# Keeping the merged sum and two branch outputs of a hybrid decoder step in DRAM, with one tile pool for both lanes and gates ahead of projections in the last branch

## The chip, the core and the metric

The kernel runs on one core of one Trainium2 chip. The core has five engines with an instruction queue each: TensorE (PE, matmuls), VectorE (DVE), ScalarE (ACT), GpSimd (POOL) and SyncE (SP, which issues most DMAs). Each queue runs in order. The metric is the device time of one execution in microseconds; several executions are timed and their median is given. One execution is profiled, and all rows below come from that one.

## What is computed

One inference step of a two-layer decoder on 512 prompt tokens and 32 sample tokens (8 sequences of 4), which share all weights. In each layer four branches read one combined projection of the normalised input; each branch output (width 512) is gated, projected to 1024 and weighted, and the four are summed:

```python
h = rmsnorm(x, norm_g); z = h @ w_in          # columns split among all branches
y_conv, y_hg, y_mla, y_mem = ...              # short conv | HGRN2 | MLA over a paged cache | memory cross-attention
ys = jnp.stack([y_conv, y_hg, y_mla, y_mem], axis=2) * jax.nn.silu(sg)
proj = jnp.einsum('btnw,nwd->btnd', ys, w_bout)
merged = jnp.sum(jax.nn.sigmoid(mg) * proj, axis=2)
return x + merged @ w_o, ...
```

The keys and values of the memory branch come from `rmsnorm(mem) @ w_k` and `@ w_v` per layer; the MLA branch of the sample tokens reads 2048 cached positions per sequence through a page table.

## The kernel before

All activations are kept feature-major: 128 features on the partitions, 544 tokens (512 + 32) in the free dimension, in two halves of 272. Every large product is done in three float32r matmuls: a weight is split into `wh` (ACT copy) and `wl` (DVE subtract), an activation into a high and a low part (`Hh`/`Hl`, `ysh`/`ysl`, `Mh`/`Ml`), and high-high, high-low and low-high are accumulated.

The work of TensorE is a list of **items**, one weight tile each (`add`, `zi`): four `mk` and four `mv` (keys and values of the memory), then per layer the latent tiles, the queries, the conv tiles, and per branch four gates `sg` and eight pairs of `mg` (the gate of the merge) and `pj` (the projection), at last eight `wo`. A z item is 48 matmuls of 128x272, a `pj` 24. The three tiles of an HGRN head (hq, hf, hi) are put between pairs: heads 0 and 1 in the conv branch, heads 2 and 3 in the memory branch (`HG`). Counted from 0, item 57 is hq of head 2, items 68 to 70 are hq, hf and hi of head 3, and big matmul 2784 of the first layer is the first of item 70.

The main loop loads item i+2, splits item i+1, runs the deferred calls, runs the matmuls of item i with a step of **lane** a between its halves, evacuates its PSUM tile and makes a step of lane b. Lane a holds memory attention and HGRN, lane b MLA; both are generators whose small matmuls (`sm`, four PSUM tiles) fill in between the big ones (`big`, two PSUM tiles, so that item i+2 needs item i copied out). `drain` runs a lane to the point that an item needs.

Program order is not the final order: a scheduler moves instructions on each engine, and tiles come from rotating pools, so that an instruction which writes a new tile waits until an older tile of that pool is free. Pools here: `wrp` (3 raw weight tiles), `whp` (2 of `wh`, 2 of `wl`), `ep` (3 tiles e), `tpa` (13 tiles for lane a) and `tpb` (14 for lane b), and `kp` with single tiles, among them `M` (8 x 544, the merged sum, which also serves as X, the residual stream) and `ym`.

The places that the change touches: `ev_pj` makes the merged sum: the conv branch writes `M` on DVE, the others add to it on POOL. `split_merged` makes `Mh` and `Ml` from `M` ahead of the first `wo` item. `ev_out` adds the residual into X, stores it to DRAM (`x1`) for the next layer, and `xn_feed` squares and adds it for the norm; `xn_finish` gets the norm's factor (a short chain on POOL), makes the tiles e, and splits them into `Hh` and `Hl`. `mem_load` and `mem_split` load the memory rows and split them (`ra`) for `mk` and `mv`. The outputs of memory attention are in `ym`, those of HGRN in one lane tile per head, until the `sg` items gate them. For the sample tokens of MLA, eight jobs per quarter load the cached latents (`tb<-in_latT`, four DMAs each), split them into `rb` and run their small matmuls; those with `S`, `m`, `QR` and `cnew` belong to their softmax.

Of the kernel before, what the change touches and what calls it, by code (L numbers as in the profile page):

```python
# [19 lines left out]
P = 128  # L20
# [18 lines left out]
TA, TB = 13, 14  # L39
# [97 lines left out]
def hybrid_kernel(ctx: ExitStack, tc: tile.TileContext, a, o):  # L137
# [7 lines left out]
    ep = pool("ep", 3)  # L145
    tps = {"a": pool("tpa", TA), "b": pool("tpb", TB)}
# [10 lines left out]
    def t(name=None):  # L157
        n = name or lane[0]
        return tps[n].tile([P, T], F32, tag="t" + n, name="t" + n)

    def tr():
        return tps[lane[0]].tile([P, T], F32R, tag="t" + lane[0], name="r" + lane[0])
# [59 lines left out]
    x1 = dp.tile([P, KD, T], F32, name="x1")  # L222

# [205 lines left out]
    def xn_finish(l):  # L429
# [6 lines left out]
        rs = rstd_small(ps[:, 0:5], 1024, alloc=sl_, eng=G)  # L436
# [10 lines left out]
        for d in range(KD):  # L447
            h = e_()
            stt(h, X[:, d, :], g_("norm", 8 * l + d), r, ALU.mult, ALU.mult)
# [178 lines left out]
    def ev_sg(l, n, i):  # L628
        def run(it):
# [10 lines left out]
            else:  # L640
                y = {CONV: lambda: st[l]["cv"], HGRN: lambda: st[l]["yh", i], MEM: lambda: st[l]["ym"][:, i, :]}[n]()
                stt(g, g, 0.5, y, ALU.mult, ALU.mult)
# [16 lines left out]
    def ev_mg(l, n, d):  # L659
        def run(it):  # L660
            x = e_()
            act(v2(x), ps2(it), AF.Tanh, scale=0.5)
            st[l]["tm"] = x
        return run

    def ev_pj(l, n, d):
        def run(it):
            x = st[l]["tm"]
            if n == CONV:
                if d == 0:  # L670
                    st[l]["M"] = kp.tile([P, KD, T], F32, tag="M", name="M")
                stt(v2(st[l]["M"][:, d, :]), v2(x), 1.0, ps2(it), ALU.add, ALU.mult)
            else:
                stt(v2(x), v2(x), 1.0, ps2(it), ALU.add, ALU.mult)
                tt(st[l]["M"][:, d, :], st[l]["M"][:, d, :], x, ALU.add, eng=G)
        return run

    def split_merged(l):
        M = st[l]["M"]
        Mh = kp.tile([P, KD, T], F32R, tag="H1", name="Mh")  # L680
        Ml = kp.tile([P, KD, T], F32R, tag="H2", name="Ml")
        for d in range(KD):
            act(Mh[:, d, :], M[:, d, :], AF.Copy)
            tt(Ml[:, d, :], M[:, d, :], Mh[:, d, :].bitcast(F32), ALU.subtract)
        st[l]["Ms"] = (Mh, Ml)

    def ev_out(l, d):
        def run(it):
            if d == 0:
                X = kp.tile([P, KD, T], F32, tag="M", name="X")  # L690
                if l + 1 < NL:
                    st[l + 1]["X"] = X
                st[l]["Xn"] = X
# [961 lines left out]
```

## Time and profile before

| | |
|---|---|
| median of 3 runs | 1739.29 us (1735.88 to 1740.36) |
| the profiled execution | 1735.38 us, of which the span is 1733.2 us |
| PE busy | 1704.0 us (98%), 14042 matmuls; weight loads 1642.6 us (95%) |
| DVE busy | 1079.2 us (62%) |
| ACT busy | 849.7 us (49%) |
| POOL busy | 333.2 us (19%) |
| DMA | 201.12 MB, 116 GB/s on average |

The span runs from the first to the last instruction; the 2.2 us that lie around it belong to the execution's time. A busy share is an average over the whole span. Where a row of the trace has an idle time in brackets, the engine stood still before that instruction, and the name behind the arrow is what ended the wait.

### The profile page before, as it was taken

Reading aid. Unit: us, or ns where it says so; the run is one execution under the profiler, and the core shown is the slowest. Engines: PE = TensorE matmul, PEld = TensorE weight load, DVE = VectorE, ACT = ScalarE, POOL = GpSimd, SP = SyncE. Lnnn points to the kernel's source line nnn. Section 1 sums busy time; section 2 is a strip of 40 time slices with the busy share of each in tenths; the row PEclk is TensorE's granted clock in tenths of the full one; section 3 lists DMA queues with packets and bytes.
Section 4 is the critical chain, followed back from the end, with each engine's and each line's share of the span. In section 5 each row is a group of like instructions: output and inputs, shape, how many; then the busy total and the mean of one; then the engine's idle time right before and its main releaser. Section 6 shows DMA issues by size and latency. Waiting matters only on the chain.

```text
span 1733.2 us, 36030 instructions
## 1 busy us (share of the span) xinstructions
PE 1704.0 (98%) x14042; PEld 1642.6 (95%) x14042; DVE 1079.2 (62%) x2468; ACT 849.7 (49%) x1651; POOL 333.2 (19%) x366
## 2 busy tenths in 40 slices
PE   7999999999999999999999999999999999999999
PEld 5899899999999999999989998999999999999999
DVE  7565654768787976332465756556787888744333
ACT  6646444565757563222346554355656665523231
POOL 5010001112243322101130100001133433221110
PEclk9999999999999999999999999999999999999999
DMA  6322542334334443223453135323343434333233
GB/s 233 116 62 77 172 132 81 106 113 128 118 120 133 132 127 105 90 74 111 153 169 106 53 98 178 105 78 115 115 141 106 143 110 128 110 101 87 83 113 121
DMA packets 106828, 201.12 MB, mean 116 GB/s; under 512 B 13921, under 2 KB 48098, under 8 KB 106658
## 3 DMA queue, kind: packets, MB, share of 16 engines
q1 hardware_dynamic: 99346, 177.79, 32.9%
q0 software_dynamic: 7168, 20.98, 4.1%
q8 instruction: 111, 1.82, 0.4%
q14 instruction: 59, 0.48, 0.1%
q10 hardware_dynamic: 144, 0.04, 0.0%
HBM read 186.72 MB, written 12.04 MB: 115 GB/s over the span
## 4 chain that ended last, share of the span: by engine, by line
PE 86%; DVE 6%; ACT 4%; issue 2%; DMA 1%; SPq 1%; POOL 0%; ACTq 0%; DVEq 0%
PE big L171 66%; PE sm L171 18%; DVE ta L180 1%; DVE wl L180 1%; DMA tb<-in_latT 1%; ACT ta L174 1%; ACT tb L174 1%; ACT wh L174 1%; DVE e L177 1%; ACT L174 1%; SPq L1244 0%; PE sm L1203 0%; PE sm L981 0%; DVE Ml L180 0%; DMA ta<-in_memT 0%
## 5 line engine op out<-in xcount | busy, mean ns | idle before, releaser
L171 PE MATMUL big<-Hh,wh 128*128 128x272 f32 x2528 | 744.3, 295 | 0.6 <-ACT Hh L174 0.2
L171 PE MATMUL big<-Hh,wl 128*128 128x272 f32 x2528 | 736.6, 291 | 2.9 <-DVE wl L180 2.9
L171 PE MATMUL big<-Hl,wh 128*128 128x272 f32 x2528 | 735.0, 291 | 2.2 <-DVE Hl L180 1.8
L171 PEld LDWEIGHTS big<-Hh,wh 128*128 128x128 f32 x2528 | 477.5, 189 | 8.7 <-issue 5.6
L171 PEld LDWEIGHTS big<-Hl,wh 128*128 128x128 f32 x2528 | 477.7, 189 | 6.2 <-DVE Hl L180 2.8
L171 PEld LDWEIGHTS big<-Hh,wl 128*128 128x128 f32 x2528 | 477.0, 189 | 5.5 <-DVE wl L180 4.3
L174 ACT ACTIVATE wh<-wr 128x1024 fp32r<-128x1024 f32 (+1 forms) x246 | 232.8, 946 | 460.2 <-PE big L171 382.3
L180 DVE TENSOR_TENSOR wl<-wr,wh 128x1024 fp32r<-128x1024 f32 (+1 forms) x246 | 273.3, 1111 | 272.2 <-ACT wh L174 271.2
L174 ACT ACTIVATE tb<-sm 128x256 f32<-128x256 f32 (+6 forms) x380 | 140.2, 398 | 81.2 <-PE sm L171 66.4
L180 POOL TENSOR_TENSOR M<-M,e 128x544 f32<-128x544 f32 x48 | 96.9, 2019 | 358.4 <-DVE e L177 349.2
L171 PE MATMUL big<-ysh,wh 128*128 128x272 f32 x512 | 149.6, 292 | 0.0
L171 PE MATMUL big<-ysh,wl 128*128 128x272 f32 x512 | 148.6, 290 | 0.0
L171 PE MATMUL big<-ysl,wh 128*128 128x272 f32 x512 | 148.4, 290 | 0.0
L174 ACT ACTIVATE ta<-ta 128x544 f32<-128x544 f32 (+3 forms) x180 | 96.0, 538 | 55.6 <-DVE ta L180 46.4
L171 PE MATMUL sm<-ta 128*128 128x128 f32 (+6 forms) x1424 | 122.5, 279 | 0.3
L180 DVE TENSOR_TENSOR ta<-ta 128x256 f32<-128x256 f32 (+3 forms) x248 | 111.9, 488 | 8.8 <-ACT ta L174 8.1
L171 PEld LDWEIGHTS sm<-ta 128*32 128x32 f32 (+1 forms) x1424 | 101.2, 147 | 9.0 <-issue 2.8
L171 PE MATMUL sm<-Rh,rb 128*128 128x272 f32 x512 | 105.9, 295 | 2.0 <-DVE S L1276 2.0
L1222 POOL DMA_INDIRECT tb<-in_rop,row4i x64 | 71.3, 1113 | 189.9 <-PE sm L171 94.9
L189 DVE TENSOR_REDUCE s<-tb 128x8 f32<-128x512 f32 (+1 forms) x150 | 100.8, 674 | 4.5 <-ACT tb L174 4.4
L1222 POOL DMA_INDIRECT tb<-in_lat,row4i x64 | 68.8, 1074 | 158.4 <-PE sm L171 63.6
L171 PEld LDWEIGHTS big<-ysh,wh 128*128 128x128 f32 x512 | 96.6, 189 | 0.4 <-issue 0.4
(242 smaller groups left out, 2556.1 us busy)
## 6 DMA issues: line engine op xcount, KB each, us to landing
wr<-in_w_in SPq DMA_DIRECT2D x158, 512.0 KB
wr<-in_wb SPq DMA_DIRECT2D x64, 256.0 KB
tb<-in_latT SPq DMA_DIRECT2D x256, 64.0 KB
ta<-in_mkT SPq DMA_DIRECT2D x32, 256.0 KB
ta<-in_mv SPq DMA_DIRECT2D x32, 256.0 KB
wr<-in_wo SPq DMA_DIRECT2D x16, 512.0 KB
ta<-in_shg SPq DMA_DIRECT2D x16, 256.0 KB
out_hgs<-ta SPq DMA_DIRECT2D x16, 256.0 KB
```

The lines of the kernel that those rows point to most:

```text
L171: return TE.matmul(out, lhsT, rhs, start=start, stop=stop)
L174: S.activation(out, in_, f, **k)
L177: V.scalar_tensor_tensor(out=out, in0=in0, scalar=sc, in1=in1, op0=op0, op1=op1)
L180: (eng or V).tensor_tensor(out=out, in0=in0, in1=in1, op=op)
L189: V.tensor_reduce(out=out, in_=in_, op=op, axis=AX.X, **k)
L1222: G.indirect_dma_start(out=out, out_offset=None, in_=a[src], in_offset=bass.IndirectOffsetOnAxis(ap=idx, axis=0))
```

## The change

The merged sum leaves the on-chip memory: it is kept in a DRAM tensor `md`. Each branch's `ev_mg` loads the sum so far into a tile e, `ev_pj` adds to it and a deferred call stores it again. The outputs of memory attention and HGRN go to DRAM too (`ymd`, `yhd`), and `load_y` fetches them ahead of the `sg` items. The tiles `M` and `ym` are gone; in their place there are six tiles e instead of three, and the two lane pools become one of 27. X is a list of eight tiles of that pool. The norm's factor is made on DVE. In the MLA branch all eight `mg` items come first, then all eight `pj` items, and each merged tile gets its last sum and its split right behind its `pj` item, so `split_merged` is gone.

```diff
-TA, TB = 13, 14
+NT = 27
...
-    ep = pool("ep", 3)
-    tps = {"a": pool("tpa", TA), "b": pool("tpb", TB)}
+    ep = pool("ep", 6)
+    lp = pool("lp", NT)
...
     def t(name=None):
         n = name or lane[0]
-        return tps[n].tile([P, T], F32, tag="t" + n, name="t" + n)
+        return lp.tile([P, T], F32, tag="t", name="t" + n)
...
+    md = dp.tile([P, KD, T], F32, name="md")
+    ymd = dp.tile([P, 4, T], F32, name="ymd")
+    yhd = dp.tile([P, 4, T], F32, name="yhd")
...
-        rs = rstd_small(ps[:, 0:5], 1024, alloc=sl_, eng=G)
+        rs = rstd_small(ps[:, 0:5], 1024, alloc=sl_)
...
-                y = {CONV: lambda: st[l]["cv"], HGRN: lambda: st[l]["yh", i], MEM: lambda: st[l]["ym"][:, i, :]}[n]()
-                stt(g, g, 0.5, y, ALU.mult, ALU.mult)
+                stt(g, g, 0.5, st[l]["y"] if n != CONV else st[l]["cv"], ALU.mult, ALU.mult)
...
     def ev_mg(l, n, d):
         def run(it):
-            x = e_()
+            x = t("b") if n == MLA else e_()
             act(v2(x), ps2(it), AF.Tanh, scale=0.5)
-            st[l]["tm"] = x
+            st[l]["tm", d] = x
+            if n != CONV:
+                m = st[l]["mo", d] = t("b") if n == MLA else e_()
+                SY.dma_start(out=m, in_=md[:, d, :])
         return run
 
     def ev_pj(l, n, d):
         def run(it):
-            x = st[l]["tm"]
-            if n == CONV:
-                if d == 0:
-                    st[l]["M"] = kp.tile([P, KD, T], F32, tag="M", name="M")
-                stt(v2(st[l]["M"][:, d, :]), v2(x), 1.0, ps2(it), ALU.add, ALU.mult)
-            else:
-                stt(v2(x), v2(x), 1.0, ps2(it), ALU.add, ALU.mult)
-                tt(st[l]["M"][:, d, :], st[l]["M"][:, d, :], x, ALU.add, eng=G)
-        return run
-
-    def split_merged(l):
...
+            x = st[l].pop(("tm", d))
+            stt(v2(x), v2(x), 1.0, ps2(it), ALU.add, ALU.mult)
+            if n != CONV:
+                tt(x, x, st[l].pop(("mo", d)), ALU.add, eng=V if n == MLA else G)
+            if n != MLA:
+                defer(1, lambda: SY.dma_start(out=md[:, d, :], in_=x))
+                return
+            if d == 0:
+                st[l]["Ms"] = (kp.tile([P, KD, T], F32R, tag="H1", name="Mh"), kp.tile([P, KD, T], F32R, tag="H2", name="Ml"))
+            Mh, Ml = st[l]["Ms"]
+            act(Mh[:, d, :], x, AF.Copy)
+            tt(Ml[:, d, :], x, Mh[:, d, :].bitcast(F32), ALU.subtract)
+        return run
 
     def ev_out(l, d):
         def run(it):
...
+            xo = t("b")
+            if l + 1 < NL:
+                st[l + 1].setdefault("X", []).append(xo)
...
-            act(ym[:, :, qb * P:(qb + 1) * P], ps.rearrange("p (h q) -> p h q", h=4), AF.Copy)
+            y = t()
+            act(y[:, 0:TP], ps, AF.Copy)
+            defer(1, lambda: SY.dma_start(out=ymd[:, :, qb * P:(qb + 1) * P], in_=y[:, 0:TP].rearrange("p (h q) -> p h q", h=4)))
...
         stt(ob, ob, g_("hgn", 4 * l + h), r, ALU.mult, ALU.mult)
-        st[l]["yh", h] = ob
+        defer(1, lambda: SY.dma_start(out=yhd[:, h, :], in_=ob))
...
+    def load_y(l, name, flag, src, i):
+        def run():
+            if i == 0:
+                drain(l, name, flag)()
+                run_deferred()
+            y = e_()
+            SY.dma_start(out=y, in_=src[:, i, :])
+            st[l]["y"] = y
+        return run
...
                 zi(l, ("mg", n, d), ev_mg(l, n, d))
-                add(l, ("pj", n, d), a["wb"][l, n, d], 512, proj_mm(l), ev_pj(l, n, d))
+                if n != MLA:
+                    add(l, ("pj", n, d), a["wb"][l, n, d], 512, proj_mm(l), ev_pj(l, n, d))
+            if n == MLA:
+                for d in range(8):
+                    add(l, ("pj", n, d), a["wb"][l, n, d], 512, proj_mm(l), ev_pj(l, n, d))
...
-        for tag in ("Q", "ym", "ysh", "ysl"):
+        for tag in ("Q", "ysh", "ysl"):
...
-        X = st[0]["X"] = kp.tile([P, KD, T], F32, tag="M", name="X0")
+        X = st[0]["X"] = [t("b") for _ in range(KD)]
```

The same matmuls stand in the new program, 12654 in both; SP has 1146 DMAs where it had 1016. What moves on the engines is shown at three places.

ACT in the memory branch, first layer, around the copy of HGRN head 3's hq (item 68) out of PSUM, `ta<-big`. In the kernel before:

```order
L174 ACTIVATE ta<-sm,epsc 128x272 x2
L174 ACT_TABLE_LOAD
L174 ACTIVATE ta<-ta 128x544
L174 ACT_TABLE_LOAD
L174 ACTIVATE ta<-ta 128x544
L174 ACTIVATE tb<-sm 128x256
L174 ACTIVATE ta<-ta 128x544
L174 ACTIVATE tb<-sm 128x256 x4
L174 ACTIVATE rb<-tb 128x512
L174 ACTIVATE wh<-wr 128x1024
L174 ACTIVATE ta<-big 128x544
L174 ACTIVATE S<-S 128x272
```

In the changed kernel; the row right ahead of these is `wh<-wr 128x1024`, the weights of item 71, whose buffer is that of item 69:

```order
L174 ACTIVATE ta<-sm,epsc 128x272
L174 ACT_TABLE_LOAD
L174 ACTIVATE ta<-ta 128x544
L174 ACT_TABLE_LOAD
L174 ACTIVATE ta<-ta 128x544 x2
L174 ACTIVATE rb<-tb 128x512
L174 ACTIVATE tb<-sm 128x256 x5
L174 ACTIVATE S<-S 128x272
L174 ACTIVATE rb<-tb 128x512
L174 ACTIVATE tb<-sm 128x256 x4
L174 ACTIVATE tb<-sm 128x128
L174 ACTIVATE ta<-big 128x544
```

The copy stood behind the weights of item 70, and stands now behind those of item 71, the norm of the head before (the two table loads) and the ACT rows of two latent jobs. The second layer has the same.

PE at the same place. In the kernel before, `big<-Hh,wh` in the seventh row is the first matmul of item 70, and 9 small matmuls stand between it and item 69:

```order
L171 MATMUL sm<-Rh_105,rb 128x272 x2
L171 MATMUL sm<-Rl_107,rb 128x272
L171 MATMUL sm<-Rh_105,rb 128x272 x2
L171 MATMUL sm<-Rl_107,rb 128x272
L171 MATMUL sm<-Rh_105,rb 128x272 x2
L171 MATMUL sm<-Rl_107,rb 128x272
L171 MATMUL big<-Hh,wh 128x272
L171 MATMUL big<-Hl,wh 128x272
```

In the changed kernel 46 small matmuls stand between the two, of which these are the last 27, and then item 70:

```order
L171 MATMUL sm<-Rl_104,rb 128x272
L171 MATMUL sm<-m,ones 128x16
L171 MATMUL sm<-tb,S 32x128 x16
L171 MATMUL sm<-cnew,S 32x128
L171 MATMUL sm<-Rh_102,rb 128x272 x2
L171 MATMUL sm<-Rl_104,rb 128x272
L171 MATMUL sm<-Rh_102,rb 128x272 x2
L171 MATMUL sm<-Rl_104,rb 128x272
L171 MATMUL sm<-Rh_102,rb 128x272 x2
L171 MATMUL sm<-Rl_104,rb 128x272
L171 MATMUL big<-Hh,wh 128x272
L171 MATMUL big<-Hl,wh 128x272
```

The small matmuls are the same ones; those that stood among the big matmuls of items 66 to 69 have gathered ahead of item 70. At item 59 there is a shorter such run, of 15.

ACT at the layer change, where the last output items are followed by `mk` and `mv` of the second layer (`e<-X` or `e<-tb` is the square for the norm). In the kernel before:

```order
L174 ACTIVATE e<-X 128x544
L174 ACTIVATE wh<-wr 128x1024
L174 ACTIVATE e<-X 128x544
L174 ACTIVATE wh<-wr 128x1024 x4
L174 ACTIVATE ta<-big,rmem 128x512
L174 ACTIVATE tb<-big,rmem 128x512
```

In the changed kernel:

```order
L174 ACTIVATE e<-tb 128x544
L174 ACTIVATE wh<-wr 128x1024
L174 ACTIVATE e<-tb 128x544
L174 ACTIVATE ra<-ta,gn 128x256 x8
L174 ACTIVATE wh<-wr 128x1024 x3
L174 ACTIVATE tb<-sm 128x512
```

The split of the memory rows, `ra<-ta,gn`, which stood in the HGRN branch, has moved behind the square of the last X tile; its low parts, on DVE, likewise stand behind that tile's addition and a `wl`.

## Rows read from the trace of the kernel before

**Rows 1.** The page: busy time by engine, DMA bytes, the chain by line.
```profile
PE 1704.0 (98%) x14042; PEld 1642.6 (95%) x14042; DVE 1079.2 (62%) x2468; ACT 849.7 (49%) x1651; POOL 333.2 (19%) x366
...
DMA packets 106828, 201.12 MB, mean 116 GB/s; under 512 B 13921, under 2 KB 48098, under 8 KB 106658
...
PE big L171 66%; PE sm L171 18%; DVE ta L180 1%; DVE wl L180 1%; DMA tb<-in_latT 1%; ACT ta L174 1%; ACT tb L174 1%; ACT wh L174 1%; DVE e L177 1%; ACT L174 1%; SPq L1244 0%; PE sm L1203 0%; PE sm L981 0%; DVE Ml L180 0%; DMA ta<-in_memT 0%
```

**Rows 2.** Waits of PE: waiting line, releaser, us in total, times, longest.
```profile
PE big L171 <- ACT ra L174: 6.8, 1, 6.8
...
PE sm L171 <- DVE S L1276: 2.0, 2, 1.7
```

**Rows 3.** Windows: length, busy us (instructions) by engine, granted clock, DMA share, GB/s.
```profile
26.20:33.00 6.80, 6.75 (x21) 5.79 (x22) 3.90 (x8) 1.01 (x2) 5.19 (x17) 0.50 0.36 139
...
510.00:560.00 50.00, 50.00 (x424) 49.45 (x423) 39.43 (x110) 32.26 (x64) 16.96 (x20) 1.00 0.51 149
```

**Rows 4.** Timeline of ACT at items 68 and 69: start, us, instruction, [idle before].
```profile
525.08 1.07 ACT L174 ACTIVATE ta<-sm,epsc 128x272 f32<-128x272 f32 x2 [0.32 <-PE sm L171]
526.17 1.28 ACT L174 ACT_TABLE_LOAD   x1
527.46 0.66 ACT L174 ACTIVATE ta<-ta 128x544 f32<-128x544 f32 x1
528.14 1.28 ACT L174 ACT_TABLE_LOAD   x1
...
530.81 1.34 ACT L174 ACTIVATE tb<-sm 128x256 f32<-128x256 f32 x4
532.05 0.62 ACT L174 ACTIVATE rb<-tb 128x512 fp32r<-128x512 f32 x1
532.57 1.05 ACT L174 ACTIVATE wh<-wr 128x1024 fp32r<-128x1024 f32 x1
533.52 0.61 ACT L174 ACTIVATE ta<-big 128x544 f32<-128x544 f32 x1
...
539.56 0.28 ACT L174 ACTIVATE tb<-sm 128x128 f32<-128x128 f32 x1 [3.21 <-PE sm L171]
```

**Rows 5.** Timeline of DVE in the same stretch.
```profile
534.35 0.43 DVE L180 TENSOR_TENSOR S<-S,sm 128x272 f32<-128x272 f32 x1
...
536.43 0.62 DVE L189 TENSOR_REDUCE m<-S 128x16 f32<-128x272 f32 x1
```

**Rows 6.** Timelines at the layer change: PE, ACT, DVE.
```profile
875.49 0.63 PE L171 MATMUL big<-wh,ra 128*128 128x512 f32 x2
...
876.58 0.64 ACT L174 ACTIVATE e<-X 128x544 f32<-128x544 f32 x1
...
875.69 0.72 DVE L177 SCALAR_TENSOR_TENSOR X<-big,e 128x544 f32<-128x544 f32 x1 [3.80 <-PE big L171]
876.70 1.23 DVE L180 TENSOR_TENSOR wl<-wr,wh 128x1024 fp32r<-128x1024 f32 x1 [0.29 <-ACT wh L174]
```

**Rows 7.** Timelines of ACT and DVE in the HGRN branch: the split of memory.
```profile
621.82 0.90 ACT L174 ACTIVATE ra<-ta,gn 128x256 fp32r<-128x256 f32 x2
...
623.89 0.48 DVE L177 SCALAR_TENSOR_TENSOR ra<-ta,gn,ra 128x256 fp32r<-128x256 f32 x1
```

**Rows 8.** Timelines of PE and DVE at the first output item.
```profile
829.48 0.40 PE L171 MATMUL big<-Ml,wh 128*128 128x272 f32 x1 [0.78 <-DVE Ml L180]
...
826.90 4.42 DVE L180 TENSOR_TENSOR Ml<-M,Mh 128x544 fp32r<-128x544 f32 x5
```

**Rows 9.** Timeline of PE at the start.
```profile
24.62 0.73 PE L171 MATMUL big<-wh,ra 128*128 128x512 f32 x2 [2.00 <-ACT wh L174]
26.25 1.01 PE L171 MATMUL sm<-ones,tb 128*128 128x1 f32 x4 [0.89 <-DVE tb L180]
```

**Rows 10.** Pieces of the chain, in order of time: start, us, what.
```profile
469.94 3.24 DMA tb<-in_latT
...
700.43 45.24 PE big L171 x360
```

More of the change, by code (lines that the diff above doesn't have):

```diff
@@ L158, in t @@
         n = name or lane[0]
-        return tps[n].tile([P, T], F32, tag="t" + n, name="t" + n)
+        return lp.tile([P, T], F32, tag="t", name="t" + n)
     def tr():
-        return tps[lane[0]].tile([P, T], F32R, tag="t" + lane[0], name="r" + lane[0])
+        return lp.tile([P, T], F32R, tag="t", name="r" + lane[0])
     e_ = lambda: ep.tile([P, T], F32, tag="e", name="e")
@@ L448, in xn_finish @@
             h = e_()
-            stt(h, X[:, d, :], g_("norm", 8 * l + d), r, ALU.mult, ALU.mult)
+            stt(h, X[d], g_("norm", 8 * l + d), r, ALU.mult, ALU.mult)
             act(Hh[:, d, :], h, AF.Copy)
@@ L712, in lane_a @@
         KT, Vt = st[l]["KT"], st[l]["Vt"]
-        ym = st[l]["ym"] = kp.tile([P, 4, T], F32, tag="ym", name="ym")
         def p_s(qb):
@@ L831, in lane_a @@
         TE.transpose(ps[:, 0:P], acc[:, 0:P], ident)
-        act(ym[:, :, TP:T], ps[:, 0:P].rearrange("p (h t) -> p h t", h=4), AF.Copy)
+        y = t()
+        act(y[:, 0:P], ps[:, 0:P], AF.Copy)
+        SY.dma_start(out=ymd[:, :, TP:T], in_=y[:, 0:P].rearrange("p (h t) -> p h t", h=4))
         st[l]["mem_done"] = True
@@ L1457, in hybrid_kernel, with branch @@
             zi(l, ("sg", CONV, i), ev_sg(l, CONV, i))
-        def branch(n, before=None, after=None):
+        def branch(n, before=None):
             for d in range(8):
@@ L1476, in hybrid_kernel @@
         for d in range(8):
-            add(l, ("wo", d), a["wo"][l, d], 1024, out_mm(l), ev_out(l, d), pre=(lambda l=l: split_merged(l)) if d == 0 else None)
+            add(l, ("wo", d), a["wo"][l, d], 1024, out_mm(l), ev_out(l, d))
         if l + 1 < NL:
@@ L1533, in hybrid_kernel @@
         load(3)
-        X = st[0]["X"] = kp.tile([P, KD, T], F32, tag="M", name="X0")
+        X = st[0]["X"] = [t("b") for _ in range(KD)]
         for d in range(KD):
-            SY.dma_start(out=X[:, d, :], in_=a["xT"][:, d, :])
+            SY.dma_start(out=X[d], in_=a["xT"][:, d, :])
         for i in range(4, 8):
@@ L1542, in hybrid_kernel @@
         for d in range(KD):
-            defer(1 + d // 2, lambda d=d: xn_feed(0, d, X[:, d, :]))
+            defer(1 + d // 2, lambda d=d: xn_feed(0, d, X[d]))
         defer(2, setup)
```

17 lines of the change are left out of this document (2 added, 15 removed).

## Prediction

> **What bounds the kernel now.** I read the page first [rows 1]: TensorE (PE) is busy 1704.0 of 1733.2 us, and the chain that ended last is 66% big and 18% small matmuls, so only some 29 us of the span are not matmuls. The list of PE's waits [rows 2] says where: 6.8 us before the first one, then small change, among it two for the sample scores `S`; the split of the merged sum, `Ml`, makes two more [rows 8]. A page like this says that an edit can gain little, and that it costs whatever new waits it puts into PE's order. Nor does the diff touch what PE computes: the matmuls are the same in number and shape. So I went through the order of the instructions for places where PE must now wait for something that used to be early, and costed each from the timeline of the stretch in which it stood before.
>
> **Part 1, one tile pool: an evacuation that comes late (term A).** In the memory branch the three gates of HGRN head 3 (hq, hf, hi) are items 68, 69 and 70. The two big PSUM buffers alternate, so item 70 can't start before item 68 has been copied out, by ScalarE (ACT) into a tile of lane a. In the kernel before, that copy is the row at 533.52, a microsecond after item 69's start freed the weights of the wh at 532.57, and the whole stretch is dense: PE is busy 50.00 of 50.00 us [rows 3, 4]. In the changed kernel the order shows ACT's copy (`ta<-big`) twelve rows later, behind the norm of the head before and the ACT work of two paged-attention jobs, and PE's row shows the counterpart: 46 small matmuls in a row stand between the end of item 69 and item 70, where before it was nine. The tile that the copy writes now comes from the pool that both lanes share; whatever the reason, both queues run in order, so item 70 waits for that copy.
>
> How long? The first ACT row of the group is a wh that needs item 69's buffer, so nothing of it starts before PE has finished item 69; call this T. From below, ACT's own work: wh 1.06, half of the pair at 525.08 (0.5), two table loads 2.56, three `ta<-ta` of 0.66, two rb of 0.62, nine tb at 1.34 for four (3.0), 0.28 and the copy 0.61 make 11.2; neighbours overlap by some 0.1 each, so about 10 [rows 4]. The 46 matmuls fill part of it: 33 of 272 columns at 0.126 (45.24 us for 360, [rows 10]), 17 of 128 at half of that, a few tiny ones: 5.3 us. That leaves 4.7. From the other side, the same chain was run in the kernel before, hidden: from the norm's scaling at 525.08 to `tb<-sm` at 539.56 + 0.28 it took 14.8 us, because the steps go back and forth: ACT to VectorE (DVE; the add into S at 534.35, the maximum at 536.43), to PE (ACT's last row waited 3.21 for it) and back [rows 4, 5]. The first 0.5 of this lies ahead of T and the copy's 0.6 comes on top, 14.9; less 5.3 is 9.6. In the chain before, PE's big matmuls and a wl held it up by perhaps 2, and a wh of 1 and an rb of 0.7 are now in it that weren't, so I take 9.0, near the measured chain, with 4.7 and 12 as ends (12 if the latent load of the last job, which now stands behind a weight load that itself waits for item 69's buffer, is the later one: 2.3 for the weights, about 2 to issue, 3.24 to land [rows 10], then 1.3 of splitting, some 9 us, so it should be just hidden). Both layers have the place: **A = +18 (9.4 to 24)**.
>
> The same happens on a small scale at item 57 (hq of head 2): 15 small matmuls ahead of item 59, the copy behind a wh and one tb. After T that is 1.06 + 0.33 + 0.61 = 2.0 of ACT against 1.65 of PE, plus PSUM hand-offs: 1.5 each, **B = +3.0 (0.8 to 8)**. And the first loads of the cached memory keys stand behind the stores of the memory output: a store waits for its copy, then 0.3 to issue and 3.24 to land [rows 10], against some 3.4 us of matmuls up to the first use: 1.2 each, **C = +2.4 (0 to 6)**.
>
> **Part 2, the layer change (term D).** Before, the memory rows of the second layer were loaded and split in the HGRN branch (ACT at 621.82, DVE at 623.89 [rows 7]), and PE went from the last output matmul straight into `big<-wh,ra` at 875.49 [rows 6]. Now the tiles come free only with the last output items: the split stands behind X7 and its square on ACT (end 877.2) and behind X7 and a wl on DVE (end 877.9) [rows 6]. The first half of ra takes 0.45 more on ACT, its low part 0.48 on DVE [rows 7]: second matmul at 878.4, a stall of 2.7. Then the six h tiles ahead of Hl, which six e buffers allow, push two wl of 1.23 behind them; by the same rows PE waits 1.5 and 3.2 there, but the waits of before in this stretch (2 us) and 2 us of the norm, now on DVE instead of GpSimd (POOL), come back: **D = +3.2 (1 to 9)**.
>
> **Part 3, what it gains.** The split of each merged tile follows its projection, so the `Ml` waits go: PE stood 0.78 in front of one [rows 8] and some 0.4 in front of another, 1.2 per layer. DVE has five of them in one run of 4.42 us there [rows 8]; spread over the projections it needs 0.72 + 0.71 + 0.71 + 0.68 = 2.8 per 3.0 us of PE, nearly full, so I keep 1.0 each: **E = -2.0 (-2.5 to +0.5)**. At the start the norm leaves POOL and the squares no longer wait for e buffers; the last Hl comes about 2 us earlier, though the first ra now stands behind two more wh: **F = -2.0 (-4 to +2.5)**. The stores and reloads in DRAM themselves I cost at nothing: some 130 transfers of about 0.27 MB, 35 MB on 201 [rows 1], each with 6 us or more of other items between landing and use; the adds stay on POOL except in the last branch.
>
> **Part 4, the clock (term G).** After waits of 2.00 and 0.89 us in a row [rows 9] the granted clock was 0.50 for 6.8 us [rows 3], half of 2.4 GHz, which cost 3.4. Nothing in the kernel before has a gap as long as the new ones of A. The Trainium skill (TensorE: Matmul & The Clock Gate, Part 1: The HAM clock gate) has half rate as the state of an idle engine, lifted by activity; the rows at the start agree (0.50), and by it each of the two waits of A would be followed by a full spell, +6.8 in all. In A the PE is not idle but runs small matmuls in bursts, and its half clock is partly hidden behind the same chain, so I take 2 for each: **G = +4 (0 to 10, with the layer change)**.
>
> The small waits for S and the like shift with the small matmuls (2.0 us over two places [rows 2]); I take **H = -1 (-4 to +4)**.
>
> **Sum.** 18 + 3.0 + 2.4 + 3.2 - 2.0 - 2.0 + 4 - 1 = +25.6 on the profiled execution's 1735.38 us, so 1761.0. That execution lies 3.9 us below the median of the three runs (1739.29), and the changed kernel is timed like the median: 1739.3 + 25.6 = 1764.9, **about 1765 us**.
>
> **The rivals.**
> (1) Not slower: the long run of small matmuls is no wait. If ACT and DVE were well ahead when PE reaches T (because PE had already been held up earlier), the copy would come right after the run. Against it: the wh at the head of the group needs item 69's buffer, and ACT's own 10 us stand behind it. It would take A down to at most its lower end, 9.4, with B, C and G at zero, D at 1, E and F at -6.5 and H at -4: 1739 or a little less. It decides the sign from A below some 4 to 5 us per layer on. 0.08.
> (2) Faster: the shared pool and the six e buffers let the lanes run ahead, the run of 46 costs nothing, and the waits beyond the first 6.8 [rows 2] go in part. What is there to be had is 29 - 6.8 = 22 us at most, plus the half clock at the start; a third of it gives 1731. Against it: PE was dense already in the stretches where the lanes are heaviest [rows 3]. 0.04.
> (3) Much slower: the 130 DMAs more on SP's queue, which are in order and wait for POOL adds, hold the latent loads behind them; each job then adds its landing [rows 10] to PE's wait. Four more such waits of 3.3 us per layer give 1791. For it: in the second half of the memory branch four latent loads stand directly behind one weight load. Against: they are issued during the wait of A itself. 0.10.
> (4) Slower clock: after both waits of A and at the layer change a spell like the one at the start [rows 3] follows, and nothing hides it: G = 3 x 3.4 = 10.2, 1771. For it: each of these waits is as long as the 2.9 us at the start or longer, give or take 0.2. Against: PE works in between, and ACT and DVE catch up meanwhile. 0.20. It is what the page on TensorE named above, in the Trainium skill, would have.
>
> **How the numbers follow.** Forecast 0.58: with A between 5 and 12 per layer and the rest around the values above, 1750 to 1781, in which rival 4 lies too. Rivals 1 and 2 and most of rival 3 lie outside, so about 0.8 is held: range **1750 to 1781**. A measurement of this kernel can tell some 0.3% (5.2 us) from no change: faster 0.04 (rival 2), the same 0.07 (most of rival 1), slower 0.89.
>
> **What would show it.** A: in the profile after, PE's list of waits has two groups (near 545 and near 1410 us) in which waits for ACT copies (`tb`, `ta`), S and m stand between small matmuls, together 8 to 11 us each, and the copy `ta<-big` stands right ahead of item 70. If PE is dense there, A is wrong and with it the sign. D: a wait of some 2.7 us for ra at the layer change. E: no wait for `Ml`. G: a granted clock near 0.5 behind these waits. F: the last `Hl` before 52 us. If the time comes out slower with PE dense at A, rival 3 has to show as waits for tb and rb elsewhere in the branches.

## The result and the profile after

The changed kernel takes 1776.88 us (median of four runs, 1775.55 to 1779.11), the kernel before on the same chip 1737.72: a ratio of 1.0225, 95% interval 1.0205 to 1.0246. It is slower by 39 us in the median and by 44 in the two profiled executions.

The page of the kernel after, busy times and DMA:

```profile
span 1777.3 us, 36288 instructions
PE 1718.1 (97%) x14042; PEld 1654.8 (93%) x14042; DVE 1092.0 (61%) x2502; ACT 863.9 (49%) x1659; POOL 289.6 (16%) x326
DMA packets 129390, 236.79 MB, mean 133 GB/s; under 512 B 17025, under 2 KB 55298, under 8 KB 129218
```

Against [rows 1] the span has grown by 44.1 us. PE has the same 14042 matmuls and is busy 14.1 us longer, so they ran at a lower clock for a time (the granted clock is 0.986 on average, where it was 0.997); and it stands still for 59.2 us instead of 29.2. The waits of PE in the kernel after (engine, what it waited for, total us, times, longest us), to be held against [rows 2]:

```profile
PE big L171 <- DVE wl L180: 17.4, 10, 4.1
PE sm L171 <- DVE S L1277: 14.4, 5, 6.2
PE big L171 <- ACT ra L174: 14.0, 2, 11.7
PE big L171 <- ACT e L174: 3.7, 4, 1.4
PE big L171 <- DVE Hl L180: 2.6, 2, 1.5
PE big L171 <- DVE ra L177: 1.5, 2, 1.1
```

Four things are new: two waits of 6.2 us for `S`, a first matmul at 11.7 us instead of 6.8, long waits for `wl`, and waits for `e`; `Ml` [rows 8] is gone. To see where the 44 us lie, I took the start of each big matmul (they are the same 10080 in the same order) in both traces and compared stretch by stretch:

| big matmuls | what is there | longer by, us | predicted |
|---|---|---|---|
| up to 840 | start, first memory reads of layer 1 (F, half of C) | 5.7 | -0.8 |
| 840 to 4656 and 5600 to 9696 | branches of both layers (A, B, G, H, half of C) | 13.0 + 17.0 | 25.2 |
| 4656 to 4720, 9696 to 9760 | split of the merged tiles (E) | -2.5 | -2.0 |
| 4720 to 5600 | layer change (D) | 10.5 | 3.2 |
| sum | | 43.8 | 25.6 |

These are two single executions, and not all parts are equally sure. The runs below that leave a place as it is in the kernel after (1, 3, 8, 9 and 10 for the start, 1, 3, 8 and 9 for the layer change) show 2.6 to 6.0 us up to 840 and 8.3 to 9.8 us at the layer change; the loss from 2592 to 3300, which holds term A, is 11.5 to 12.1 us in the first layer in the runs that keep it (1, 4, 6 and 10).

**Term A in the rows.** PE after item 69 (start, us, form, idle before it and what ended the idle):

```profile
546.65 0.29 PE L171 MATMUL sm<-Rl,rb 128*128 128x272 f32 x1
553.12 1.97 PE L171 MATMUL sm<-QR,tb 128*128 128x64 f32 x8 [6.19 <-DVE S L1277]
554.88 0.55 PE L171 MATMUL sm<-m,ones 128*128 128x16 f32 x2
...
560.88 0.29 PE L171 MATMUL big<-Hh,wh 128*128 128x272 f32 x1
```

The last of these rows is item 70; from item 69 to it the trace has 79 small matmuls, nine in the kernel before. And ACT in the same stretch:

```profile
544.81 1.05 ACT L174 ACTIVATE wh<-wr 128x1024 fp32r<-128x1024 f32 x1
...
546.32 1.28 ACT L174 ACT_TABLE_LOAD   x1
...
548.28 1.28 ACT L174 ACT_TABLE_LOAD   x1
549.58 1.34 ACT L174 ACTIVATE ta<-ta 128x544 f32<-128x544 f32 x2
...
551.35 1.19 ACT L174 ACTIVATE tb<-sm 128x256 f32<-128x256 f32 x4
...
559.75 0.28 ACT L174 ACTIVATE tb<-sm 128x128 f32<-128x128 f32 x1 [0.98 <-PE sm L171]
559.92 0.62 ACT L174 ACTIVATE ta<-big 128x544 f32<-128x544 f32 x1
```

The copy of item 68 (`ta<-big`, at 533.52 in [rows 4]) now comes at 559.92, behind the norm with its table loads and the work of the jobs, and item 70 starts 0.3 us after it has ended. PE's wait is named after `S`, but what it waited for is this chain: `tb<-sm`, which frees the small PSUM tiles, stands behind the table loads. The same wait returns at 1432 us in the second layer. By stretch (us; busy time and instructions of PE, PEld, DVE, ACT, POOL; granted clock; DMA share; GB/s):

```profile
550.00:552.00 2.00, 0.00 (x0) 0.00 (x0) 0.98 (x2) 1.97 (x6) 0.00 (x0) 0.86 0.61 186
552.00:553.00 1.00, 0.00 (x0) 0.00 (x0) 1.00 (x4) 0.53 (x2) 0.00 (x0) 0.50 0.06 21
...
556.00:557.00 1.00, 1.00 (x6) 1.00 (x5) 0.59 (x2) 1.00 (x3) 0.00 (x0) 0.50 0.87 307
...
558.00:559.00 1.00, 1.00 (x24) 0.97 (x27) 0.69 (x4) 0.47 (x2) 0.00 (x0) 0.86 0.38 120
...
1429.00:1438.00 9.00, 5.73 (x32) 5.67 (x36) 6.72 (x18) 5.30 (x14) 0.00 (x0) 0.50 0.40 124
```

The granted clock falls to 0.50 (1.2 GHz) while PE stands still, stays there while it works through most of the small matmuls, and is back at 2.4 GHz before item 70. The last row is the second layer: there it is low for longer, 10 us in all instead of 7, behind a wait of the same 6.19 us.

**A second late evacuation.** At items 62 and 64 PE waits for the copies of the gates two items earlier, 1.35 and 0.5 us, and then 2.2 us for a `wl`. ACT and PE at the first of these:

```profile
479.03 1.28 ACT L174 ACT_TABLE_LOAD   x1
480.32 0.62 ACT L174 ACTIVATE e<-big 128x544 f32<-128x544 f32 x1
```

```profile
481.00 0.39 PE L171 MATMUL big<-Hh,wh 128*128 128x272 f32 x1 [1.35 <-ACT e L174]
```

The copy stands behind a table load of lane a, though the tile e that it writes doesn't come from the shared pool.

**The layer change** [rows 6, 7]. PE in the kernel after:

```profile
895.39 0.49 PE L171 MATMUL big<-wh,ra 128*128 128x512 f32 x1 [2.25 <-ACT ra L174]
896.95 0.79 PE L171 MATMUL big<-wh,ra 128*128 128x512 f32 x1 [1.07 <-DVE ra L177]
...
917.45 0.50 PE L171 MATMUL big<-wl,ra 128*128 128x512 f32 x1 [1.07 <-DVE wl L180]
...
924.57 0.80 PE L171 MATMUL big<-wl,ra 128*128 128x512 f32 x1 [4.05 <-DVE wl L180]
```

Ahead of the third of these rows, DVE has:

```profile
911.36 4.26 DVE L177 SCALAR_TENSOR_TENSOR e<-tb,gn 128x544 f32<-128x544 f32 x6
...
916.18 1.22 DVE L180 TENSOR_TENSOR wl<-wr,wh 128x1024 fp32r<-128x1024 f32 x1
```

PE stands 3.3 us for `ra`, then twice for `wl`, the first of which DVE makes behind six h tiles in a row. **The start:** ACT has two more `wh` ahead of the first `ra`, and the second of them waits for its weights:

```profile
10.20 1.06 ACT L174 ACTIVATE wh<-raw 128x1024 fp32r<-128x1024 f32 x1 [2.35 <-DMA raw<-in_wk]
11.16 2.49 ACT L174 ACTIVATE ra<-ta,gn 128x256 fp32r<-128x256 f32 x6
```

### The profile page after: what moved, and what is told of

It is laid out like the page before. It is cut to its first block, busy times and chain, and to the rows that moved or that the text cites. A ratio compares the mean times of both kernels' runs of the same rounds, so it can differ in the third digit from the quotient of the medians.

```text
span 1777.3 us, 36288 instructions
## 1 busy us (share of the span) xinstructions
PE 1718.1 (97%) x14042; PEld 1654.8 (93%) x14042; DVE 1092.0 (61%) x2502; ACT 863.9 (49%) x1659; POOL 289.6 (16%) x326
## 4 chain that ended last, share of the span: by engine, by line
PE 88%; ACT 5%; DVE 4%; issue 2%; DMA 1%; SPq 0%; DVEq 0%; ACTq 0%
PE big L171 67%; PE sm L171 19%; ACT L174 1%; ACT ta L174 1%; DVE wl L180 1%; ACT wh L174 1%; DVE e L177 1%; DVE ta L180 1%; ACT tb L174 1%; PE sm L1204 0%; PE sm L739 0%; PE sm L982 0%; DMA raw<-in_wk 0%; PE sm L1285 0%; PE sm L784 0%
## 5 line engine op out<-in xcount | busy, mean ns | idle before, releaser
L171 PEld LDWEIGHTS big<-Hh,wh 128*128 128x128 f32 x2528 | 478.9, 189 | 11.3 <-issue 4.6
L180 DVE TENSOR_TENSOR wl<-wr,wh 128x1024 fp32r<-128x1024 f32 (+1 forms) x248 | 279.5, 1127 | 245.8 <-ACT wh L174 242.6
L171 PE MATMUL sm<-Rh,rb 128*128 128x272 f32 x512 | 109.7, 301 | 0.0
L174 ACT ACTIVATE ta<-sm 128x512 f32<-128x512 f32 (+5 forms) x130 | 53.8, 429 | 99.3 <-PE sm L171 50.5
L171 PEld LDWEIGHTS big<-ysh,wl 128*128 128x128 f32 x512 | 96.4, 188 | 3.5 <-DVE wl L180 3.5
L180 POOL TENSOR_TENSOR e<-e 128x544 f32<-128x544 f32 x32 | 61.4, 1919 | 226.0 <-DVE e L177 186.9
```

The lines of the kernel that those rows point to most:

```text
L171: return TE.matmul(out, lhsT, rhs, start=start, stop=stop)
L174: S.activation(out, in_, f, **k)
L180: (eng or V).tensor_tensor(out=out, in0=in0, in1=in1, op=op)
```

## The experiments

Three theories stood against each other. **O:** with one pool, the instructions that write new tiles of both lanes come out in the order in which the program asks for the tiles, so that one lane stands behind the other. (That the scheduler goes by this order is inferred; the runs test what follows from it.) **S:** 27 tiles are too few for both lanes and X. **R:** the stores and reloads in DRAM hold up SP's queue. Ratios are to the kernel before, run on the same chip as each experiment.

| kernel | median, us | ratio (95% interval) |
|---|---|---|
| after | 1776.9 | 1.0225 (1.0205 to 1.0246) |
| after, 36 tiles | 1772.7 | 1.0208 (1.0191 to 1.0225) |
| after, two lane pools | 1735.3 | 0.9997 (0.9987 to 1.0006) |
| after, two lane pools, three e | 1733.2 | 0.9982 (0.9973 to 0.9991) |
| after, pool for the gates' copies | 1759.5 | 1.0139 (1.0122 to 1.0157) |
| after, X in its own tile | 1764.2 | 1.0163 (1.0146 to 1.0180) |
| after, both of these | 1747.3 | 1.0070 (1.0054 to 1.0085) |
| after, pool for the norm's tiles | 1779.8 | 1.0240 (1.0218 to 1.0263) |
| after, filler matmuls | 1772.3 | 1.0210 (1.0193 to 1.0227) |
| after, last branch in pairs | 1780.7 | one run, no interval |
| before, one pool | 1762.4 | 1.0156 (1.0140 to 1.0172) |
| before, one tile from the other pool | 1734.6 | 0.9992 (0.9983 to 1.0002) |
| before, last branch changed | 1732.4 | 0.9983 (0.9974 to 0.9992) |

**1. More tiles.**

```diff
-NT = 27
+NT = 36
```

> The changed kernel with 36 tiles in the one pool instead of 27. Theory O (handing out): the two lanes' tiles come from one pool in the order in which the program asks for them, whatever the number, so the copy of item 68 stays behind the ACT work of the paged-attention jobs and the rows ra stay behind X: 1777 us, give or take 3, with the same wait of some 6.2 us before the first matmul of item 70 in both layers and the first matmul near 11.7 us. Rival S (scarcity): 27 slots are too few for both lanes and eight X tiles; with nine more the late copy and the late split go, 1777 - 26 (stretch of items 68 to 70) and up to - 16 more (start, layer change): 1735 to 1751. Rival R (traffic): the stores and reloads in DRAM and their place in SP's queue hold PE up; nothing changes, 1777.

Nothing moved: 1.0208 against 1.0225, within the intervals; PE's longest waits are 6.1 us for `S` and 11.3 for `ra`. Nine tiles more, a third, buy nothing that can be told from noise, so S falls.

**2. Two lane pools, all else as in the change.**

```diff
-    lp = pool("lp", NT)
+    tps = {"a": pool("tpa", 13), "b": pool("tpb", 16)}
```

> The changed kernel with two lane pools again (13 tiles for lane a, 16 for lane b with the X tiles); DRAM copies, six tiles e, the norm on DVE and the order of the last branch stay. Theory O: all that was lost hangs on the shared pool: 26 us at items 68 to 70 (both layers), some 6 at the start and 7 to 10 at the layer change go, the gain at the last branch (2.4) stays: 1733 us (1728 to 1742), not slower than the kernel before. Rival S: 13 slots for a lane are fewer than 27 for both, so nothing is better: 1770 or more. Rival R: the DRAM traffic stays, so most of the loss stays: 1760 or more.

0.9997: the whole loss is gone with the shared pool, while the 35 MB of extra DMA stay. R falls. (The two pools hold 29 tiles and not 27; by run 1 the number is not what counts.) PE's waits in this kernel:

```profile
PE big L171 <- ACT ra L174: 6.9, 1, 6.9
PE big L171 <- DVE wl L180: 6.1, 7, 3.2
```

There is one wait for `ra`, at the start, and none of the long ones for `S`. The 3.2 for `wl` is the one behind the six h tiles; run 12 comes back to it.

**3. A pool for the copies of the HGRN gates** (hq, hf, hi); everything else shares.

```diff
-            x = t()
+            x = hp.tile([P, T], F32, tag="h", name="ta")
...
+    hp = pool("hp", 6)
```

> The changed kernel in which the tiles of the HGRN gates (copies of the hq, hf and hi items) alone come from a pool of their own, six tiles. Theory O: the copy of item 68 is early again, PE is dense in front of item 70, and only this goes: 26 us of the wait and the half clock behind it, 1751 us (1747 to 1756); the start (first matmul at 11.7) and the layer change stay as in the changed kernel. Of the 26, 12.4 are the two waits of 6.2 and the rest the clock: if the clock is low there for another reason than the wait (bursts of small matmuls), only 12 to 15 go and the time is 1763. Rival S: six more tiles help everywhere a little, also at the start: no single place to be seen. Rival R: 1777.

The place is gone, as O says: the stretch from big matmul 2592 to 3300 takes 138.9 us, where the kernel after has 150.8 and the kernel before 139.2. But the total falls by 15 us and not by 26, because part comes back later. The two rows of this kernel (columns as above) hold the stretch and the one behind it:

```profile
500.96:639.86 138.90, 137.43 (x1251) 135.60 (x1249) 108.54 (x270) 82.63 (x173) 51.61 (x46) 1.00 0.50 152
639.86:834.40 194.54, 192.20 (x1588) 190.44 (x1587) 96.50 (x182) 68.39 (x116) 22.84 (x20) 1.00 0.44 136
```

And in the kernel after:

```profile
504.08:654.85 150.77, 142.22 (x1267) 140.08 (x1266) 112.28 (x278) 89.22 (x185) 51.41 (x51) 0.98 0.47 142
654.85:844.44 189.59, 189.59 (x1572) 188.28 (x1571) 92.18 (x174) 62.71 (x105) 20.93 (x19) 1.00 0.44 138
```

11.9 us are won in the first stretch and 5.0 lost in the second: 16 small matmuls more stand there, and PE waits 2.3 us for `ysh`. The waits at items 62 and 64 stay (4.0 us), though the copy of item 57 too has a tile of the new pool here.

**4. X in a tile of its own**, as in the kernel before.

```diff
-        X = st[0]["X"] = [t("b") for _ in range(KD)]
+        X0 = kp.tile([P, KD, T], F32, tag="M", name="X0")
+        X = st[0]["X"] = [X0[:, d, :] for d in range(KD)]
...
-            xo = t("b")
+            xo = st[l]["Xn"][:, d, :]
```

> The changed kernel with X in a tile of its own again, as in the kernel before; the lanes still share 27 tiles. Theory O: the rows ra no longer stand behind the eight X tiles, so the first matmul comes near 7 us again and 5 to 6 us go at the start; at the layer change the split of ra moves forward by some twelve ACT instructions only and 0 to 6 of the 10.5 us go; items 68 to 70 stay as they are (6.2 us each, 26 in all): 1768 us (1764 to 1773). Rival S: eight slots are free for the lanes, so the wait in front of item 70 goes too: 1742 to 1748. Rival R: 1777.

As O said: the first matmul comes at 6.8 us, the start loses nothing, items 68 to 70 stay as they are. The layer change loses 1.3 us instead of 10.5, more than I had expected of it, so both places hang on the X tiles in the shared pool.

**5. Both together,** with 24 tiles for the lanes and four for the gates' copies; beside 3 and 4:

```diff
-NT = 27
+NT = 24
...
+    hp = pool("hp", 4)
```

> The changed kernel with X in a tile of its own and the copies of the HGRN gates in a pool of their own (four tiles); everything else of both lanes still shares one pool (24 tiles, fewer than before, to make room). Theory O with two separate places: both big losses go together, the start and the layer change by X (15 us in the profile of that run) and items 68 to 70 by the gates' pool (26 us, of which some come back as later small matmuls and waits for ysh): 1743 us (1737 to 1752). If the places are not independent (one wait hides the other), the time lies above 1752.

1747.3 us: of 1.0225, 3 alone takes 0.0086 and 4 alone 0.0062, and together they take 0.0155. They add up, so these are two separate places.

**6. The kernel before with one pool** and nothing else.

```diff
-    tps = {"a": pool("tpa", TA), "b": pool("tpb", TB)}
+    lp = pool("lp", 27)
```

> The kernel before with one change: both lanes take their tiles from one pool of 27. No DRAM copies, X in its own tile, the norm on GpSimd, the last branch in pairs. Theory O (the shared pool alone costs the time): items 68 to 70 lose 13 us in each layer (7.7 us idle, 5.3 by the lower clock), and items 57 to 59 some 2.6 to 3 of idle; the start stays (first matmul near 7 us), and the layer change loses 1 to 2: 26 + 1 to 9 over the kernel before, 1765 us (1758 to 1772). Rival R (DRAM copies in SP's queue are needed for the loss): within 5 us of the kernel before.

1.0156, and the traces agree in the place: two waits of 6.1 us for `S` at items 69 to 70, and the waits at items 62 and 64 as in the kernel after. The first matmul comes at 6.6 us, since X has its own tile.

```profile
PE sm L171 <- DVE S L1276: 13.7, 4, 6.1
PE big L171 <- DVE wl L180: 9.6, 8, 2.2
PE big L171 <- ACT ra L174: 6.6, 1, 6.6
```

The shared pool alone makes 27 of the 39 us; with the X tiles in it (run 4 against the kernel after) it makes 11 more.

**7. One tile moved.** In the kernel before, only the copy of item 68 takes its tile from the other lane's pool.

```diff
-            x = t()
+            x = t("b") if which == "hq" and h == 3 else t()
```

> The kernel before (two lane pools) with one tile moved: the copy of item 68 (hq of head 3) takes its tile from lane b's pool instead of lane a's. In its ACT order that copy stands six rows later, right behind the last copy of the paged-attention jobs ahead of it in the program, as in the changed kernel; the jobs themselves are not moved. Theory O with two links (with one pool the jobs stand behind the norm of the head before, and the copy behind the jobs): one link alone costs little, PE's order is as before: within 4 us of the kernel before. Simple theory (that copy standing late on ACT is the whole cost): 26 us more, 1761.

That copy then stands six rows later on ACT, and it costs nothing (0.9992). A late place in ACT's queue is not enough: in this kernel the small matmuls of the jobs still stand ahead of the end of item 69, so PE has other work while ACT gets to the copy. In the kernel after they stand behind it.

**8. The norm's tiles in a pool of their own**, so that the jobs no longer stand behind the table loads.

```diff
-        v, y, z = t(), t(), t()
+        v, y, z = (np_.tile([P, T], F32, tag="n", name="ta") for _ in range(3))
...
+    np_ = pool("np", 6)
```

> The changed kernel in which the three tiles of the norm (the chain with the two table loads) come from a pool of their own, six tiles; the gates' copies and the jobs still share one pool. In its ACT order the copies of the jobs no longer stand behind the table loads, the copy of item 68 still behind the jobs (45 small matmuls between items 69 and 70 instead of 46), and the copy of item 57 is early again. Theory O with two links: the first link goes, so the wait of 7.7 us shrinks by the two table loads and the steps between them (2.6 to 4 us per layer) and the 2.6 to 3.0 us of items 57 to 59 go: 8 to 14 us less than the changed kernel, 1765 (1760 to 1771). If the late copy alone makes the wait: 1771 or more.

This missed by 15 us, though not at the place itself. ACT there, and one row of the clock:

```profile
547.36 1.07 ACT L175 ACTIVATE wh<-wr 128x1024 fp32r<-128x1024 f32 x1
...
559.92 0.62 ACT L175 ACTIVATE ta<-big 128x544 f32<-128x544 f32 x1
```

```profile
558.00:560.00 2.00, 2.00 (x31) 1.50 (x20) 1.53 (x5) 0.25 (x2) 0.00 (x0) 0.50 0.49 173
```

From the `wh` at the head of the chain to the copy of item 68 it takes 12.6 us instead of 15.1, just the two table loads less; the longest wait for `S` is 2.0 us, and the stretch from 2592 to 3300 has 5.5 us of idle time instead of 8.6. But the clock is at 0.50 from 552 to 562 us behind several short waits, and the stretch is only 1.4 us shorter than in the kernel after. The loss lies ahead of it: big matmuls 840 to 2592 take 317.7 us instead of 312.6, with 1.4 us more of idle and 3.8 of busy time, and the same stretch of the second layer loses 4.4 us. The 2.6 to 3.0 us that were to go stand at items 62 to 64 and not at 57 to 59, and did not go; the clock is low there for 6.6 us instead of 3.2, and 13 small matmuls more stand in the stretch. The chain is what O says, then, but this cut of the pool moved other waits, and how much each of these costs wasn't tried.

**9. Filler matmuls in the wait,** added in the function `kn` behind the last matmul of one job; their results are not used.

```diff
+                    if (b, q, j) == (4, 1, 3):
+                        for _ in range(40):
+                            mm(ps[:, 272:512], h[:, c], R[:, 0:240])
```

> The changed kernel with 40 matmuls of 128x240 added in each layer, right behind the matmuls at which PE then waits 6.2 us for S (items 69 to 70); their results are not used. They take some 4.4 us of that wait, nothing else moves. Theory G (the lower clock behind the wait comes from PE standing still): the clock stays at its upper level in the 8 us behind, which gives back up to 5.3 us per layer: 1766 us where the changed kernel has 1777 (ratio to before 1.0164 instead of 1.0225). Rival (the lower clock comes from the small matmuls themselves, or the 5.3 us are something else): the clock falls all the same and the time is that of the changed kernel; if the added matmuls are not hidden by the wait, 9 us more.

PE in this kernel:

```profile
543.98 4.64 PE L171 MATMUL sm<-Rh,rb 128*128 128x240 f32 x40
550.34 1.10 PE L171 MATMUL sm<-QR,tb 128*128 128x64 f32 x8 [1.72 <-DVE S L1280]
...
554.60 0.39 PE L171 MATMUL sm<-m,ones 128*128 128x16 f32 x2 [1.16 <-DVE S L1280]
```

And the stretches in which the clock had been at 0.50:

```profile
552.00:553.00 1.00, 1.00 (x8) 0.86 (x8) 0.75 (x2) 0.22 (x1) 0.00 (x0) 1.00 0.44 164
...
555.00:557.00 2.00, 2.00 (x41) 1.80 (x42) 1.81 (x6) 0.76 (x2) 0.00 (x0) 1.00 0.42 122
```

The first half of theory G holds: with PE at work in the gap, the clock stays at 1.00, so the standing still had brought it down and not the small matmuls. The second half falls. The stretch from 2592 to 3300 takes 150.0 us instead of 150.8 (151.5 to 150.0 in the second layer), and a new wait of 1.16 us for `S` stands where PE was slow before. The chain on ACT and DVE ends when it ends; the low clock was hidden behind it, but for 0.7 and 1.5 us. The median is 4.6 us below that of the kernel after and not the 11 expected, the intervals overlap, and 4.7 of the 6.9 us between the two profiled executions lie at the start and the layer change, which the filler doesn't touch.

**10. The last branch in pairs again.**

```diff
-                if n != MLA:
-                    add(l, ("pj", n, d), a["wb"][l, n, d], 512, proj_mm(l), ev_pj(l, n, d))
+                add(l, ("pj", n, d), a["wb"][l, n, d], 512, proj_mm(l), ev_pj(l, n, d))
```

> The changed kernel with the last branch in pairs of gate and projection again, as the other branches. Theory (term E hangs on the order): the tiles Mh and Ml can only be written when the last gate has read Hh and Hl, so the split of all eight tiles comes in one run at the end and PE waits for Ml again, 1.2 us per layer: some 2.4 us more than the changed kernel's 1773 to 1777, of which the profile shows the waits. If splitting at once makes the gain and not the order, no wait for Ml.

One run, 1780.7 us. The split comes in one run again and PE waits at this place, 2.3 us per layer, though for a `tb` and not for `Ml`. Seen from big matmul 4600 to 4700, it is 3.9 us worse than the kernel after in the first layer. So the gain needs the order, as far as one run can say; that the order works by freeing `Hh` and `Hl` for `Mh` and `Ml` is argued from the program and not shown.

**11. The kernel before with only the last branch changed**, the merged sum on the chip.

```diff
+            if n == MLA:
+                for d in range(8):
+                    add(l, ("pj", n, d), a["wb"][l, n, d], 512, proj_mm(l), ev_pj(l, n, d))
...
+                act(Mh[:, d, :], M, AF.Copy)
+                tt(Ml[:, d, :], M, Mh[:, d, :].bitcast(F32), ALU.subtract)
...
-    def split_merged(l):
```

> The kernel before with only the last branch changed: eight gates, then eight projections, the add on DVE and each merged tile split at once; the merged sum stays in its tile on the chip, two lane pools. If term E is right, the waits for Ml (0.91 us in one stretch of some 8 us, 1.2 in all, in each layer) go and nothing else moves: 2.4 us less than the kernel before, ratio 0.9986, some 1733 us. Rival: DVE is nearly full in the projections (2.8 of 3.0 us) and the gain turns into waits for wl: ratio 1.000 or above.

0.9983, 2.7 us: the gain of term E by itself, 1.2 us per layer in the trace. This kernel beats both.

**12. Two lane pools and three tiles e,** on top of 2.

```diff
-    ep = pool("ep", 6)
+    ep = pool("ep", 3)
```

> The changed kernel with two lane pools again (13 and 16 tiles) and three tiles e instead of six. Theory D (at the layer change six h tiles in a row, which six tiles e allow, push a wl back): with three tiles only three h tiles stand ahead of the wl, the wait of 3.2 us in front of big matmul 5114 goes down to the 0.6 of the kernel before, and the time is 2 to 2.5 us less than with six tiles e (ratio 0.9997 then): ratio 0.9984, some 1733 us. Rival: with the loads of the merged sum and of the branch outputs three tiles e are too few, and PE waits for those loads in the branches: ratio above 1.000.

0.9982. The wait for `wl` at the layer change, with the h tiles that DVE makes ahead of it, first with six tiles e (run 2), then with three:

```profile
889.05 5.33 DVE L177 SCALAR_TENSOR_TENSOR e<-tb,gn 128x544 f32<-128x544 f32 x6
895.64 0.79 PE L171 MATMUL big<-wl,ra 128*128 128x512 f32 x1 [3.22 <-DVE wl L180]
```

```profile
891.05 2.17 DVE L177 SCALAR_TENSOR_TENSOR e<-tb,gn 128x544 f32<-128x544 f32 x3
898.14 0.50 PE L171 MATMUL big<-wl,ra 128*128 128x512 f32 x1 [0.60 <-DVE wl L180]
```

Three tiles e are enough for the loads from DRAM, and with two pools the change as a whole is then faster by 2.3 us.

## Why the prediction was right, and where it was not

The sign and the main cause were right; the time, 1776.9, lies at the upper end of the range and 12 us above the 1765. In the two profiled executions the sum is 18 us short: 7 at the layer change, 6.5 at the start and 5 in the branches.

**A, the late evacuation: right.** It stands where it was put (at 546 to 561 us and again at 1426 to 1440), the copy is the last ACT row ahead of item 70, and the shared pool causes it (runs 2, 3 and 6). Between big matmuls 2592 and 3300 the two layers lose 11.5 and 10.5 us, 22 together. The prediction had 18 for A and 2 for the clock at each of the two places, 22. The chain itself was right: from the end of item 69 to the end of the copy it took 15.4 us (545.2 to 560.5), where 14.9 was forecast. What PE does meanwhile was not, and that the sum fits so well is in part luck. Of the 15.7 us up to the start of item 70 PE works for 9.5 and not 5.3, since 79 small matmuls stand there and not 46 (the 33 of 272 columns and 17 of 128 that the prediction itself counted are already more), and 5.2 of the 9.5 us are at half clock; so it stands still for 6.2 us and not 9.0, in one wait and not in several of 8 to 11 us together. Another 1.5 us is a wait for `wl` further on, at 588 us, that the prediction didn't have. "Whatever the reason", the prediction said of the shared pool; runs 1 and 7 narrow it down. It is not the number of tiles, and the copy's own place in ACT's queue does not make the wait: the jobs' small matmuls must also have moved behind item 69.

**G, the clock: the kind right, the count misleading.** 0.50 stood behind the waits, and 1.00 once the gap was filled (run 9). The Trainium skill has it so (TensorE: Matmul & The Clock Gate, Part 1: The HAM clock gate): an idle engine drops to half rate, activity lifts it. PE's busy time grew by 14.1 us, far above the 4 of the sum and the 10.2 of rival 4. But run 9 shows that at A this is no cost of its own: with the full clock 0.7 and 1.5 us come back, close to the 2 each, and rival 4's "nothing hides it" was wrong there. At the layer change 5.0 of the 10.5 us are busy time, and whether they are hidden too wasn't tried. The clock was also low for 3.2 us behind the waits at items 62 to 64 (493.5 to 496.7 us) and again in the second layer, a place where the prediction had no wait and so no term.

**B and H: no wait at the place of B, others behind it.** At items 57 to 59 (big matmuls 2256 to 2400) PE doesn't stand still in the first layer, and for 0.3 us in the second, against 1.5 each. The new idle time of these stretches, 2.6 and 3.0 us, comes at items 62 to 64, from copies of gates and a `wl` that the prediction had not gone through; with two pools the waits for these copies are all but gone (run 2). In the comparison from 840 to 2592 nothing of it shows, because small matmuls moved away (PE has 2653 matmuls there in all, 2689 before) and came back later: 54 more from 3300 to 4656, 69 more from 8340 to 9000, where they cost 5.5 us. H was put at -1 for such shifts. Together with A and G the branches lost 30.0 us against 25.2.

**C: 0.3 and 0.2 us instead of 1.2 each.** No wait for these loads is to be seen; the lower end was right.

**D, the layer change: 10.5 instead of 3.2, outside its range of 1 to 9.** The waits were foreseen nearly in size: 3.3 for `ra` (2.7), 1.07 and 4.05 for `wl` (1.5 and 3.2). The waits of before that the prediction gave back went too: the idle time of the stretch grew from 3.4 to 8.9 us, 5.5, and 2.7 + 1.5 + 3.2 - 2 would have been 5.4. Two steps failed. The "2 us of the norm" gave nothing, since PE had not waited for the norm there. And the clock, for which G kept nothing at this place in its value of 4, took 5.0: it fell twice, behind the waits for `ra` (0.62 from 895 to 900 us) and behind the long one for `wl` (0.50 from 925 to 930). In runs 1, 3, 8 and 9, with the same waits here, the busy time is 2.8 to 4.6 us more than before and the loss 8.3 to 9.8, so the misses of this term are surer than their size. Run 4 shows that the loss needs the X tiles in the shared pool, run 12, with two pools, that the last wait hangs on the six tiles e.

**F, the start: +5.4 instead of -2.0, outside its range.** The prediction saw that the first `ra` stands behind two more `wh` and priced that as ACT work. It missed that the second of these waits for its own weights, 2.35 us on a load that SP issues as early as before (2.63 us, before 2.64) and that is there only at 10.2: the first matmul comes 4.9 us later, and behind the start 5.4 are lost (2.6 to 6.0 with the memory reads in the runs that leave the start alone). The other half of the term failed too: the last `Hl` ends at 55.1 us and not before 52, and in runs 2 and 4, where the first matmul is at 6.9 and 6.8 again, nothing is gained up to 840 (0.7 and -0.2 us). Run 4 takes the whole loss away. A step that is moved behind another has to be costed with what the other one waits for.

**E: right,** -1.2 us per layer, alone (run 11) as well as in the change. The DRAM copies cost nothing that can be measured, as said (run 2; run 12, too, keeps them). Rivals 1 and 2 fell with A, rival 3 with run 2.

## What to carry to other kernels

When two lanes of work share one rotating pool, tiles of one lane can end up behind the other's chain, and more tiles don't help; an output that frees PSUM should draw on a pool that no long chain uses. Read a low clock behind a wait with care: PE's busy time grows, but if a chain on other engines ends the stretch, the full clock gives little back. And a change that bundles a good part with a bad one should be taken apart: here the order of the last branch is worth some 2.5 us by itself.

## What was not expected of the hardware

With a gap of 6.2 us in PE's work the granted clock fell to 0.50 and stayed there through 5 to 7 us of small matmuls; with the same gap filled but for 1.7 and 1.2 us it stayed at 1.00 throughout, and the stretch was only 0.7 us shorter. How long it stays low is not told by the gap: behind the same 6.2 us it was low for some 7 us in the first layer of the kernel after and 10 in the second, and the other way round in run 1. Nor does it take a long gap: in run 8, with gaps of 0.3 to 1.1 us between small matmuls, it was low for 10 us in both layers.
